# A two-layer decoder trunk: weight blocks added by accumulating transfers, FFN-in by seven products over two quads, FFN-out in parts of 3, 3, 3 and 2

## The chip, the cores and the metric

The kernel runs on one core of one Trainium2 chip. The metric is device time in microseconds (us). Three runs of the kernel before took 2845.32 to 2847.76 us, with a median of 2845.46 us. The execution whose profile is read here took 2846.71 us.

The engines are named as in the profile: PE (TensorE matrix products), PEld (its weight loads), DVE (VectorE), ACT (ScalarE), POOL (GpSimd) and SP (SyncE, which here only issues transfers).

## The reference

Two layers, each on 256 tokens of width 2048:

```python
h = rms_norm(x, g_mix_pre)
proj = h @ w_in                       # 2048 x 11776: pool, conv, q, k, v, swish gate, 3 branch gates
y_pool = pool_mixer(u_pool, ...) @ w_pool_proj
y_conv = conv_module(u_conv, ...) @ w_conv_proj
y_ret = retention(q, k, v, g_ret, ...) @ w_ret_proj
merged = gates[0] * y_pool + gates[1] * y_conv + gates[2] * y_ret
x = x + rms_norm(merged @ w_out, g_mix_post)          # 2048 x 2048
h = rms_norm(x, g_ffn_pre)
a, b = jnp.split(h @ w_ffn_in, 2, axis=-1)            # 2048 x 11264
x = x + rms_norm((jax.nn.silu(a) * b) @ w_ffn_out, g_ffn_post)   # 5632 x 2048
```

All data are 32-bit floats. Nearly all the work is the products with the large weight matrices, and each weight is used once, by 256 tokens.

## The kernel before

**Tiling.** The 256 tokens are two halves (h = 0 and 1) of 128. A weight matrix is cut into chunks of 512 columns, and a chunk into k-tiles of 128 rows. One *product* multiplies one half's k-tile of activations with one k-tile of weights, 128x128 by 128x512, and adds to a PSUM bank. To keep precision, each operand is split into a rounded part and a remainder, so `product` issues three matmuls (L830, L831, L832): activations' high part by weights' high part, low by high, high by low.

**A weight block's way.** A block is two k-tiles (`LOAD`), 128x2x512 floats, 512 KB. `fetch` has SP transfer it into a `raw` buffer (six of them, `RAWBUFS`); `load` has ACT cast it to `whi` (L808) and DVE subtract to get `wlo` (L809); there are seven `whi` and seven `wlo` buffers (`WBLOCKS`). The matmuls read these. The loop at the end of `trunk` runs half 0 ahead of half 1 by up to eight k-tiles (`LAG`), and `load_ahead` loads blocks in the order of the list `items` up to seven blocks beyond where half 1 stands. So the cast of a block waits for a free `whi` buffer, that is, for the last matmul on the block seven places earlier.

**Seven products instead of eight.** For some *quads* (four k-tiles) of a pair of neighbouring chunks n and n+1, the two halves by two row pairs by two chunks form a 2x2 by 2x2 block product. Plainly that is 8 products of each of two k-tiles, 16; by the Winograd form of Strassen's rule it is 7, so 14. `mixed` names the quads, `SEVEN` the kinds of product: b11, b21 and b22 are blocks as they lie in memory, t1 to t4 sums of blocks. b12 is loaded too, but never multiplied itself. Four sums per quad are made on DVE, in place in the `raw` buffers: L788 (t1), L812 (t3), L813 (t2) and L795 (t4). Sums of the activations come from `token_sums`, a small job on DVE and ACT. The partial results are put together on DVE by L868, L870, L875 and L882 for each pair of chunks.

44 pairs of chunks use this, each on one quad: 12 pairs of gate chunks, 2 of the output projection, 20 of FFN-in, 10 of FFN-out.

**FFN.** FFN-in and FFN-out alternate in parts: 3, 4 and 4 column blocks of the hidden layer, each followed by the FFN-out products over those 12, 16 and 16 k-tiles, which add to an accumulator in SBUF (L643, L647, L648).

**Order of the work.** Within an engine the instructions run in the order of the program, which is fixed when it is built. POOL does the adding of branches (L569) and small steps of the norms; it issues no transfers. All transfers are issued by SP.

Of the kernel before, what the change touches and what calls it, by code (L numbers as in the profile page):

```python
# [18 lines left out]
P = 128  # L19
# [20 lines left out]
SLOTS = 24  # L40

# [36 lines left out]
def trunk(ctx: ExitStack, tc: tile.TileContext, x, x_cols, positions, g_mix_post, g_ffn_post, w_in, pool_w,  # L78
# [103 lines left out]
    def pre_norm_quad(h, c, gain, mixed):  # L182
        st["xT", h].append(split(transpose4(x_block(h, c)), gain[:, 4 * c:4 * c + 4]))
        if mixed and c == 3 and h == 1:
            add_sums("sum", "xT", 3)

    def token_sums(lhs, c):

        ts = [st[lhs, h][c] for h in range(2)]
        u = slot([P, 2, 4, P])  # L190
        for h in range(2):
            dve.tensor_tensor(u[:, h], ts[h][:, 0].bitcast(F32), ts[h][:, 1].bitcast(F32), op=ALU.add)
            yield 0.7
        a11, a12, a21, a22 = (u[:, h, 2 * i:2 * i + 2] for h in range(2) for i in range(2))
        s = slot([P, 4, 2, P])
        dve.tensor_tensor(s[:, 0], a21, a22, op=ALU.add)
# [3 lines left out]
        dve.tensor_tensor(s[:, 3], a12, s[:, 1], op=ALU.subtract)  # L200
# [121 lines left out]
    def add_sums(key, lhs, c):  # L322
        jobs.insert(0, [(key, 0), token_sums(lhs, c), 0, True])
# [176 lines left out]
    def ev_rot(key, qd):  # L500
        def f(h, ps):
# [25 lines left out]
            if key == "kT" and qd == 1 and h == 1:  # L527
                add_sums("sum", "xT", 3)
# [29 lines left out]
    def ev_y(b, c):  # L558
        def f(h, ps):
            g = st["sg", h, b, c]  # L560
            if b == 0:
                if c % 2 == 0:
                    st["mt", h, c // 2] = slot([P, 2, NB])
                dve.tensor_tensor(st["mt", h, c // 2][:, c % 2, :], ps, g, op=ALU.mult)
                return
            m = st["mt", h, c // 2][:, c % 2, :]
            t = t2("tb", 2)
            dve.tensor_tensor(t, ps, g, op=ALU.mult)  # L568
            gp.tensor_tensor(m, m, t, op=ALU.add)  # L569
            if b == 2:  # L570
                if c == 0:
                    st["mT", h] = []

                def put():
                    st["mT", h].append(split(transpose4(m)))
                    if h == 1 and c == 0:
                        add_sums("sum", "mT", 0)

                defer(2 * D_T, put)
        return f  # L580
# [38 lines left out]
    def ev_b(first):  # L619
        def f(h, ps, t=None):  # L620
# [9 lines left out]
            def put():  # L630
                hid.append(split(transpose4(u)))
                if first and h == 1:
                    add_sums("sum", "hid", 0)
# [38 lines left out]
    for l in range(DEPTH):  # L672
        wi = w_in[l]

        def gate(b, c, needs=()):
            add(wi, 0, 16, Q_GATE + b * D + c * NB, "xT", ev_gate(b, c), needs)
# [13 lines left out]
        for b in range(3):  # L690
            for c in (0, 2):
                mix(*GATE_QUADS[b])
                for cc in (c, c + 1):
                    gate(b, cc, ("sum", "sum2")[:len(GATE_QUADS[b])])
                for cc in (c, c + 1):
                    project(b, cc)
        for c in range(4):
            if c == 0:
                mix(0)
            add(w_out[l], 0, 16, c * NB, "mT", ev_out(l, c), ("sum",))  # L700
        ends.append(len(chunks))
        parts = ((0, 3), (3, 7), (7, 11))
        for p, (b0, b1) in enumerate(parts):
            last = p == len(parts) - 1
            for j in range(b0, b1):
                if j:
                    mix(3)
                add(w_ffn_in[l], 0, 16, j * NB, "xT", ev_a, ("sum",) if j else ())
                add(w_ffn_in[l], 0, 16, HIDDEN + j * NB, "xT", ev_b(j == b0))
            for c in range(4):  # L710
                if c == 0 or c == 2 and not last:
                    mix(0)
                add(w_ffn_out[l], b0 * 4, (b1 - b0) * 4, c * NB, "hid", ev_ffn(l, c, p, last), ("sum",))
# [14 lines left out]
    while n < len(chunks):  # L728
        ks = list(range(0, chunks[n][2], LOAD))
        if n in mixed:  # L730
            ks = [k for k in ks if k // 4 not in mixed[n]]

            head = max(LAG // LOAD, len(ks) - 1) if len(mixed[n]) == 1 else len(ks)
            for k in ks[:head]:
                plan("", n, k)
            for q in mixed[n][:-1]:
                for kind, d in SEVEN:
                    plan(kind, n, 4 * q + d)
            q = 4 * mixed[n][-1]
            plan("b11", n, q)  # L740
            plan("t1", n, q)
            for k in ks[head:]:
                plan("", n, k)
            plan("b21", n, q + 2)
            plan("b22", n, q + 2)
            for k, kind, kq in zip(ks, ("t2", "t3", "t4"), (q, q, q + 2)):
                plan("", n + 1, k)
                plan(kind, n, kq)
            for k in ks[3:]:
                plan("", n + 1, k)  # L750
# [9 lines left out]
        count[n] = len(items)  # L760
    raws = {}
# [5 lines left out]
    def fetch(i, n=None, k=None):  # L767
        if n is None:
            n, k = items[i][1:]
        w, r0, kt, c0 = chunks[n][:4]  # L770
        r = (r0 + k) * P
        raw = wpool.tile([P, LOAD, NB], F32, name=nm("raw"), tag="raw", bufs=RAWBUFS)
        step = LOAD if i else 1
        for kk in range(0, LOAD, step):
            nc.sync.dma_start(raw[:, kk:kk + step], w[r + kk * P:r + (kk + step) * P, c0:c0 + NB]
                              .rearrange("(k p) n -> p k n", p=P))
# [5 lines left out]
    def load():  # L782
# [3 lines left out]
        if kind == "t1":  # L786
            kept["b12"] = fetch(i, n + 1, k)
            dve.tensor_tensor(kept["b11"], kept["b12"], kept["b11"], op=ALU.subtract)  # L788
            raw = kept["b11"]
        elif kind == "t2":  # L790
            raw = kept["b22"]
        elif kind == "t3":
            raw = kept["b12"]
        elif kind == "t4":
            dve.tensor_tensor(kept["b21"], kept["b21"], kept["b22"], op=ALU.subtract)  # L795
            raw = kept["b21"]
        elif kind == "b22":
            raw = kept[kind] = fetch(i, n + 1, k)
        else:
# [3 lines left out]
            kept[kind] = raw  # L803
# [7 lines left out]
        if kind == "b22":  # L811
            dve.tensor_tensor(kept["b12"], raw, kept["b12"], op=ALU.subtract)  # L812
            dve.tensor_tensor(raw, raw, kept["b11"], op=ALU.subtract)  # L813
# [21 lines left out]
    def mixed_product(kind, n, k, w):  # L835

        kk, last = k % 2, k % 2 == 1 and k // 4 == mixed[n][-1]
        lhs, outs = chunks[n][4], (chunks[n][5], chunks[n + 1][5])
# [23 lines left out]
        elif kind == "b22":  # L862
            product((0, n + 1), "mm0", s_part(3), w, False)
        elif kind == "t2":
            x = bank(s_part(1))
            if last:
# [3 lines left out]
                dve.tensor_tensor(st["sum", 0, n], s, banks["t1", n], op=ALU.add)  # L870
        elif kind == "t3":
            x = bank(s_part(2))
            if last:
                s = st["sum", 1, n]
                dve.tensor_tensor(s, s, x, op=ALU.add)  # L875
        elif kind == "t4":
            y = product((1, n), "mm1", a_part(1), w, last)
            if last:
# [3 lines left out]
                dve.tensor_tensor(s, s, banks["t1", n], op=ALU.add)  # L882

    def multiply(h):
# [6 lines left out]
        else:  # L891
            w, r0, kt, c0, lhs, evac, needs = chunks[n]
            if k == (4 if mixed.get(n, mixed.get(n - 1)) == (0,) else 0):
# [158 lines left out]
```

## Time and profile before

| | |
|---|---|
| runs | 2845.32, 2845.46, 2847.76 us |
| the profiled execution | 2846.71 us, of which the span of its instructions is 2844.9 us |
| granted TensorE clock | 0.999 of full speed |
| PE busy | 2825.8 us (99%) |
| DVE busy | 2257.6 us (79%) |
| ACT busy | 1434.2 us (50%) |
| POOL busy | 104.4 us (4%) |
| read from HBM | 559.11 MB, 199 GB/s over the span with what is written |

The page of the profile gives busy times by engine, the chain of waits (the work that ended last, followed back), and groups of equal instructions, each with its line, engine, operation, `out<-in`, count, busy time, mean of one, and the idle time before it with what ended that. A matmul's record is longer than the distance between two of them, because they overlap; the pace is read from how many lie in a stretch of time.

### The profile page before, as it was taken

The page shows a single profiled execution, that of the slowest core. Times are in us where ns is not written, and L with a number is a line of the kernel's source. Part 1 is how long each engine was busy: PE and PEld are TensorE (multiplying, and loading weights), DVE is VectorE, ACT ScalarE, POOL GpSimd, SP SyncE. Part 2 cuts the span into 40 slices and gives each one's busy share as a digit, 9 for nine tenths or more (in the row PEclk, how much of TensorE's full clock was granted, in tenths as well). Part 3 has the DMA queues.
Part 4 walks back from the last instruction along what each step waited for, and adds up shares of the span by engine and source line. Part 5 has one row for each costly group of instructions (what it writes and reads, how often), then busy time and mean ns, then how long its engine had stood idle before and what let it go on. Part 6 is the DMA issues. An engine that isn't in the chain of part 4 may idle for free.

```text
span 2844.9 us, 34694 instructions
## 1 busy us (share of the span) xinstructions
PE 2825.8 (99%) x12788; PEld 2333.2 (82%) x12788; DVE 2257.6 (79%) x2671; ACT 1434.2 (50%) x1638; POOL 104.4 (4%) x102
## 2 busy tenths in 40 slices
PE   9999999999999999999999999999999999999998
PEld 7888888888888888888888888888888888888887
DVE  6987888776888887787769778787768888887886
ACT  5444544554555554454554455455555554544553
POOL 0000001100100000000000000010000000000000
PEclk9999999999999999999999999999999999999999
DMA  8665655557655665665766655655676565656654
GB/s 306 189 191 172 202 183 188 178 191 259 187 199 200 215 199 172 220 198 192 243 213 186 191 175 177 208 178 180 207 263 189 185 215 188 218 174 201 217 194 166
DMA packets 293898, 569.78 MB, mean 200 GB/s; under 512 B 18272, under 2 KB 21600, under 8 KB 293728
## 3 DMA queue, kind: packets, MB, share of 16 engines
q1 hardware_dynamic: 293728, 567.57, 61.8%
q8 instruction: 100, 1.64, 0.2%
q14 instruction: 70, 0.57, 0.1%
HBM read 559.11 MB, written 8.39 MB: 199 GB/s over the span
## 4 chain that ended last, share of the span: by engine, by line
PE 96%; DVE 3%; ACT 0%; POOL 0%; issue 0%; DMA 0%; SPq 0%; DVEq 0%; POOLq 0%; ACTq 0%
PE mm L832 31%; PE mm L831 31%; PE mm L830 31%; PE tp L143 2%; DVE wlo L809 1%; ACT whi L808 0%; DVE slot L245 0%; PE tp L444 0%; DVE slot L137 0%; DMA raw<-in_w_in 0%; DVE ta L134 0%; DVE ta L464 0%; PE sc L408 0%; PE sc L452 0%; PE sc L434 0%
## 5 line engine op out<-in xcount | busy, mean ns | idle before, releaser
L808 ACT CAST whi<-raw 128x1024 fp32r<-128x1024 f32 (+1 forms) x1157 | 1200.7, 1052 | 1188.3 <-PE mm L831 842.7
L809 DVE TENSOR_TENSOR wlo<-raw,whi 128x1024 fp32r<-128x1024 f32 (+1 forms) x1157 | 1407.7, 1235 | 408.1 <-ACT whi L808 393.1
L830 PE MATMUL mm<-whi,slot 128*128 128x512 f32 x4008 | 1570.4, 392 | 1.2 <-ACT whi L808 0.7
L832 PE MATMUL mm<-wlo,slot 128*128 128x512 f32 x4008 | 1562.5, 390 | 3.6 <-DVE wlo L809 3.5
L831 PE MATMUL mm<-whi,slot 128*128 128x512 f32 x4008 | 1561.4, 390 | 0.7 <-DVE slot L137 0.6
L832 PEld LDWEIGHTS mm<-wlo,slot 128*128 128x128 f32 x4008 | 752.3, 188 | 164.0 <-DVE wlo L809 7.7
L830 PEld LDWEIGHTS mm<-whi,slot 128*128 128x128 f32 x4008 | 752.6, 188 | 155.5 <-ACT whi L808 3.7
L831 PEld LDWEIGHTS mm<-whi,slot 128*128 128x128 f32 x4008 | 752.9, 188 | 154.8 <-DVE slot L137 2.7
L365 DVE SCALAR_TENSOR_TENSOR slot<-slot,par,slot 128x237 f32<-128x237 f32 (+25 forms) x240 | 98.1, 461 | 0.5
L137 DVE TENSOR_TENSOR slot<-tp,slot 128x512 fp32r<-128x512 f32 x60 | 40.8, 685 | 47.4 <-ACT slot L136 47.4
L136 ACT CAST slot<-tp 128x512 fp32r<-128x512 f32 x60 | 35.2, 586 | 84.3 <-PE tp L143 84.3
L569 POOL TENSOR_TENSOR slot<-slot,tb 128x512 f32<-128x512 f32 x32 | 52.9, 1658 | 413.9 <-DVE tb L568 404.7
L237 POOL TENSOR_SCALAR ms_o<-ssq_t 128x1 f32<-128x1 f32 x8 | 1.5, 192 | 1472.8 <-DVE ssq_t L235 1472.8
L788 DVE TENSOR_TENSOR raw<-raw,raw 128x1024 f32<-128x1024 f32 x44 | 53.8, 1223 | 1.3
L813 DVE TENSOR_TENSOR raw<-raw,raw 128x1024 f32<-128x1024 f32 x44 | 53.7, 1221 | 0.9
L812 DVE TENSOR_TENSOR raw<-raw,raw 128x1024 f32<-128x1024 f32 x44 | 53.6, 1218 | 0.3
L795 DVE TENSOR_TENSOR raw<-raw,raw 128x1024 f32<-128x1024 f32 x44 | 53.6, 1218 | 0.2
L625 DVE TENSOR_TENSOR ta<-dt,mm 128x512 f32<-128x512 f32 x40 | 27.3, 683 | 21.5 <-PE mm L832 21.5
L143 PEld LDWEIGHTS tp<-ident,ta 128*128 128x128 f32 x272 | 33.8, 141 | 9.6 <-issue 1.1
L136 ACT CAST slot<-ta 128x512 fp32r<-128x512 f32 x40 | 24.8, 619 | 32.9 <-DVE ta L134 27.6
L143 PE MATMUL tp<-ident,ta 128*128 128x128 f32 x272 | 40.7, 272 | 0.3 <-DVE ta L379 0.2
L148 ACT ACTIVATE tb<-slot 128x512 f32<-128x512 f32 x48 | 30.0, 626 | 21.7 <-DVE slot L648 14.9
(136 smaller groups left out, 948.7 us busy)
## 6 DMA issues: line engine op xcount, KB each, us to landing
raw<-in_w_in SPq DMA_DIRECT2D x367, 512.0 KB, 4.0
raw<-in_w_ffn_in SPq DMA_DIRECT2D x352, 512.0 KB, 4.6
raw<-in_w_ffn_out SPq DMA_DIRECT2D x176, 512.0 KB, 4.7
raw<-in_w_out SPq DMA_DIRECT2D x64, 512.0 KB, 4.4
raw<-in_w_ret_proj SPq DMA_DIRECT2D x32, 512.0 KB, 5.5
raw<-in_w_pool_proj SPq DMA_DIRECT2D x16, 512.0 KB, 5.5
raw<-in_w_conv_proj SPq DMA_DIRECT2D x16, 512.0 KB, 5.7
x<-slot SPq DMA_DIRECT2D x12, 512.0 KB, 4.4
```

The source lines that it names most:

```text
L136: act.copy(t[:, 0], src)
L143: pe.transpose(tp[:, j, :], src[:, j * P:(j + 1) * P], ident)
L365: dve.scalar_tensor_tensor(acc[:, ct, s:], hT[:, ct, :SEQ - s], w[:, TAPS - 1 - s:TAPS - s], acc[:, ct, s:], op0=ALU.mult, op1=ALU.add)
L788: dve.tensor_tensor(kept["b11"], kept["b12"], kept["b11"], op=ALU.subtract)
L795: dve.tensor_tensor(kept["b21"], kept["b21"], kept["b22"], op=ALU.subtract)
L808: act.copy(hi[:, kk:kk + step], raw[:, kk:kk + step])
L809: dve.tensor_tensor(lo[:, kk:kk + step], raw[:, kk:kk + step], hi[:, kk:kk + step].bitcast(F32), op=ALU.subtract)
L812: dve.tensor_tensor(kept["b12"], raw, kept["b12"], op=ALU.subtract)
L813: dve.tensor_tensor(raw, raw, kept["b11"], op=ALU.subtract)
L830: pe.matmul(ps, a[0], w[0], start=first, stop=False)
L831: pe.matmul(ps, a[1], w[0], start=False, stop=False)
L832: pe.matmul(ps, a[0], w[1], start=False, stop=stop)
```

## The change

1. **Sums of weight blocks by transfers.** The four DVE subtractions and the separate load of b12 go. Signs in the block product are turned so that every sum is an addition, and each is made by a transfer from memory that adds to the `raw` buffer in place (`accum_op=ALU.add`), issued by POOL right after the block's `wlo` subtraction. b11's buffer becomes t1, then t2, then t4 by three additions one after the other; b22's buffer becomes t3 by one. `ADDED` says which block of memory is added: (chunk to the right, rows down). The order of the kinds in `items` is new too: b11 and b22 are loaded early, t1, t3, t2 and t4 later.
2. **FFN-in over two quads.** The 20 mixed pairs of FFN-in use quads 2 and 3 (`mix(2, 3)`) in place of quad 3 alone. The results of both quads add up in the same PSUM banks, so the number of combining steps per pair stays.
3. **FFN in parts of 3, 3, 3 and 2.** FFN-out's first three parts use the seven products for both of their pairs of chunks, over quad 0; the last part has none. That is 12 mixed pairs of FFN-out in place of 10.
4. The bank of t3 is read only at t2, with the other combining steps; `token_sums` is finished when the first product of b22 needs it.

```diff
-        if mixed and c == 3 and h == 1:
-            add_sums("sum", "xT", 3)
+        if mixed and c >= 2 and h == 1:
+            add_sums("xT", c)
...
-        parts = ((0, 3), (3, 7), (7, 11))
+        parts = ((0, 3), (3, 6), (6, 9), (9, 11))
...
                 if j:
-                    mix(3)
+                    mix(2, 3)
...
-                if c == 0 or c == 2 and not last:
+                if c % 2 == 0 and not last:
                     mix(0)
...
-    SEVEN = (("b11", 0), ("t1", 0), ("b21", 2), ("b22", 2), ("t2", 0), ("t3", 0), ("t4", 2))
+    ADDED = {"b11": (1, 0), "t1": (1, 2), "t2": (0, 2), "b22": (1, 0)}
...
+            head = LAG // LOAD + 1 - len(quads)
             for k in ks[:head]:
                 plan("", n, k)
+            seven("b11")
+            for k in ks[head:-1]:
+                plan("", n, k)
+            seven("b22")
+            for k in ks[max(head, len(ks) - 1):]:
+                plan("", n, k)
+            seven("t1", "b21", "t3")
+            for i, k in enumerate(ks):
                 plan("", n + 1, k)
+                if i == 0:
+                    seven("t2")
+                if i == min(2, len(ks) - 1):
+                    seven("t4")
...
-        if kind == "t1":
-            kept["b12"] = fetch(i, n + 1, k)
-            dve.tensor_tensor(kept["b11"], kept["b12"], kept["b11"], op=ALU.subtract)
-            raw = kept["b11"]
-        elif kind == "t2":
-            raw = kept["b22"]
-        elif kind == "t3":
-            raw = kept["b12"]
-        elif kind == "t4":
-            dve.tensor_tensor(kept["b21"], kept["b21"], kept["b22"], op=ALU.subtract)
-            raw = kept["b21"]
+        if kind in ("t1", "t2", "t3", "t4"):
+            raw = kept[{"t3": "b22"}.get(kind, "b11"), k // 4]
...
-        if kind == "b22":
-            dve.tensor_tensor(kept["b12"], raw, kept["b12"], op=ALU.subtract)
-            dve.tensor_tensor(raw, raw, kept["b11"], op=ALU.subtract)
+        if kind in ADDED:
+            right, down = ADDED[kind]
+            gp.dma_start(raw, block(n + right, k - k % 4 + down), accum_op=ALU.add)
```

How the change moves instructions, at three places. The numbers behind the names tell one buffer's use from another.

DVE, in a mixed pair of FFN-in of the first layer, before: `raw_9928` is b11, `raw_9949` b12, `raw_10023` b22; L625, L627, L137 and L192 are evacuations and token sums.

```order
L809 TENSOR_TENSOR wlo_9931<-raw_9928,whi_9930 128x1024
L788 TENSOR_TENSOR raw_9928<-raw_9949,raw_9928 128x1024
L625 TENSOR_TENSOR ta_9946<-dt_9650,mm_9793 128x512
L812 TENSOR_TENSOR raw_9949<-raw_10023,raw_9949 128x1024
L627 SCALAR_TENSOR_TENSOR ta_9946<-ta_9946,rstd_6091,sg_9823 128x512
L809 TENSOR_TENSOR wlo_9953<-raw_9928,whi_9952 128x1024
L809 TENSOR_TENSOR wlo_9972<-raw_9969,whi_9971 128x1024
```

The same engine and stage of the changed kernel: `raw_9097` and `raw_9116` are the two quads' b11, here as t1; `raw_9123` and `raw_9151` their b22, here as t3; `raw_9214` and `raw_9220` are b21, `raw_9173` and `raw_9275` plain blocks.

```order
L811 TENSOR_TENSOR wlo_9176<-raw_9173,whi_9175 128x1024
L811 TENSOR_TENSOR wlo_9193<-raw_9097,whi_9192 128x1024
L811 TENSOR_TENSOR wlo_9210<-raw_9116,whi_9209 128x1024
L811 TENSOR_TENSOR wlo_9217<-raw_9214,whi_9216 128x1024
L811 TENSOR_TENSOR wlo_9223<-raw_9220,whi_9222 128x1024
L811 TENSOR_TENSOR wlo_9227<-raw_9123,whi_9226 128x1024
L811 TENSOR_TENSOR wlo_9231<-raw_9151,whi_9230 128x1024
L811 TENSOR_TENSOR wlo_9278<-raw_9275,whi_9277 128x1024
```

DVE only makes `wlo` blocks here; the additions of weight blocks have left its queue.

POOL, in a mixed pair of FFN-in of the changed kernel (before, POOL has no row in these pairs): the eight accumulating transfers of one pair, with the semaphores each waits for. DMAHW are SP's transfers, DMASW POOL's own earlier ones.

```order
L816 DMA raw_7882<-in_w_ffn_in 128x2x512 [waits DMAHW2_49,DMASW2_49,DVE_49]
L816 DMA raw_7889<-in_w_ffn_in 128x2x512 [waits DMAHW3_49,DMASW3_49,DVE_49]
L816 DMA raw_7896<-in_w_ffn_in 128x2x512 [waits DMAHW4_49,DMASW7_49,DMAHW6_49,DMASW6_49,DVE_49]
L816 DMA raw_7939<-in_w_ffn_in 128x2x512 [waits DMAHW5_49,DMAHW7_49,DMAHW1_49,DVE_49]
L816 DMA raw_7882<-in_w_ffn_in 128x2x512 [waits DMASW4_49,DVE_49]
L816 DMA raw_7889<-in_w_ffn_in 128x2x512 [waits DMASW5_49,DVE_49,Activation_49]
L816 DMA raw_7882<-in_w_ffn_in 128x2x512 [waits DMASW0_49,DVE_49]
L816 DMA raw_7889<-in_w_ffn_in 128x2x512 [waits DMASW1_49,DVE_49]
```

Each waits for DVE (the `wlo` of the block it is to add to), and the three on one buffer follow each other.

ACT, in the first pair of FFN-out's second part, before: `raw_8943` is b11, then t1; `raw_8984` and `raw_9013` are a plain block and b21; `raw_9032` is b22, then t2.

```order
L808 CAST whi_8945<-raw_8943 128x1024
L808 CAST whi_8967<-raw_8943 128x1024
L808 CAST whi_8986<-raw_8984 128x1024
L136 CAST slot_9002<-tp_8997 128x512
L808 CAST whi_9015<-raw_9013 128x1024
L855 COPY dt_9008<-mm_8990 128x512
L808 CAST whi_9034<-raw_9032 128x1024
```

The same engine in the second pair of FFN-out's second part of the changed kernel: `raw_8868` is b11, t1, t2 and t4 in turn, `raw_8875` b22 and then t3, `raw_8923` b21; `raw_8959`, `raw_8984` and `raw_8990` are plain blocks of the right-hand chunk.

```order
L810 CAST whi_8870<-raw_8868 128x1024
L810 CAST whi_8877<-raw_8875 128x1024
L810 CAST whi_8902<-raw_8868 128x1024
L810 CAST whi_8925<-raw_8923 128x1024
L860 COPY dt_8918<-mm_8907 128x512
L810 CAST whi_8942<-raw_8875 128x1024
L810 CAST whi_8961<-raw_8959 128x1024
L810 CAST whi_8979<-raw_8868 128x1024
L810 CAST whi_8986<-raw_8984 128x1024
L810 CAST whi_8992<-raw_8990 128x1024
L810 CAST whi_8996<-raw_8868 128x1024
```

Between b11 and t1 there now stands one other block on ACT, between t1 and t2 three, and between t2 and t4 two; each of these distances now holds an accumulating transfer.

More of the change, by code (lines that the diff above doesn't have):

```diff
@@ L617, in ev_a, with ev_b @@
         st["sg", h] = s
-    def ev_b(first):
+    def ev_b(first, last):
         def f(h, ps, t=None):
@@ L631, in put @@
                 hid.append(split(transpose4(u)))
-                if first and h == 1:
-                    add_sums("sum", "hid", 0)
+                if first and h == 1 and not last:
+                    add_sums("hid", 0)
             defer(D_T, put)
@@ L673, in trunk, with gate @@
         wi = w_in[l]
-        def gate(b, c, needs=()):
-            add(wi, 0, 16, Q_GATE + b * D + c * NB, "xT", ev_gate(b, c), needs)
+        def gate(b, c):
+            add(wi, 0, 16, Q_GATE + b * D + c * NB, "xT", ev_gate(b, c))
         def project(b, c):
@@ L693, in trunk @@
                 for cc in (c, c + 1):
-                    gate(b, cc, ("sum", "sum2")[:len(GATE_QUADS[b])])
+                    gate(b, cc)
                 for cc in (c, c + 1):
@@ L760, in trunk @@
         count[n] = len(items)
+    first = {}
+    for i, (kind, n, k) in enumerate(items):
+        if not kind:
+            first.setdefault(n, i)
     raws = {}
@@ L765, in trunk, with block, fetch @@
     done = [0, 0]
-    def fetch(i, n=None, k=None):
-        if n is None:
-            n, k = items[i][1:]
+    def block(n, k, kk=0, count=LOAD):
         w, r0, kt, c0 = chunks[n][:4]
-        r = (r0 + k) * P
+        r = (r0 + k + kk) * P
+        return w[r:r + count * P, c0:c0 + NB].rearrange("(k p) n -> p k n", p=P)
+    def fetch(i):
+        kind, n, k = items[i]
+        n += kind == "b22"
         raw = wpool.tile([P, LOAD, NB], F32, name=nm("raw"), tag="raw", bufs=RAWBUFS)
@@ L774, in fetch @@
         for kk in range(0, LOAD, step):
-            nc.sync.dma_start(raw[:, kk:kk + step], w[r + kk * P:r + (kk + step) * P, c0:c0 + NB]
-                              .rearrange("(k p) n -> p k n", p=P))
+            nc.sync.dma_start(raw[:, kk:kk + step], block(n, k, kk, step))
         raws[i] = raw
@@ L837, in mixed_product @@
         kk, last = k % 2, k % 2 == 1 and k // 4 == mixed[n][-1]
+        if kind == "b22" and not kk:
+            finish({("sum", chunks[n][4], k // 4)})
         lhs, outs = chunks[n][4], (chunks[n][5], chunks[n + 1][5])
@@ L869, in mixed_product @@
                 st["sum", 0, n] = t2("dt", 2)
[L870 to L875, printed above, removed]
+                dve.tensor_tensor(st["sum", 0, n], banks["t1", n], s, op=ALU.subtract)
+                dve.tensor_tensor(s, s, banks["t3", n], op=ALU.add)
         elif kind == "t4":
@@ L892, in multiply @@
             w, r0, kt, c0, lhs, evac, needs = chunks[n]
-            if k == (4 if mixed.get(n, mixed.get(n - 1)) == (0,) else 0):
+            if i == first[n]:
                 finish({(s, q) for s in needs for q in (0, h)})
```

49 lines of the change are left out of this document (20 added, 29 removed).

## The prediction

> **What bounds the kernel now.** I read the page first: busy times, then the chain of waits, then a stretch of pure FFN-in by windows.
>
> ```profile
> PE 2825.8 (99%) x12788; PEld 2333.2 (82%) x12788; DVE 2257.6 (79%) x2671; ACT 1434.2 (50%) x1638; POOL 104.4 (4%) x102
> PE 96%; DVE 3%; ACT 0%; POOL 0%; issue 0%; DMA 0%; SPq 0%; DVEq 0%; POOLq 0%; ACTq 0%
> L830 PE MATMUL mm<-whi,slot 128*128 128x512 f32 x4008 | 1570.4, 392 | 1.2 <-ACT whi L808 0.7
> L831 PE MATMUL mm<-whi,slot 128*128 128x512 f32 x4008 | 1561.4, 390 | 0.7 <-DVE slot L137 0.6
> L832 PE MATMUL mm<-wlo,slot 128*128 128x512 f32 x4008 | 1562.5, 390 | 3.6 <-DVE wlo L809 3.5
> ```
>
> 96% of the chain is PE, and the three matmul groups waited 5.5 us together. So PE's number of matmuls sets the time, and DVE at 79% is next. The means of 390 ns overlap; the pace comes from counting matmuls in a stretch. The windows view, of instructions that touch the PSUM tile mm (columns: stretch, length, PE, PEld, DVE, ACT, clock, DMA share, GB/s):
>
> ```profile
> 1100.00:1200.00 100.00, 100.00 (x443) 82.81 (x442) 14.32 (x21) 1.15 (x2) 1.00 0.65 216
> ```
>
> 443 matmuls in 100 us at full clock is 0.2257 us each.
>
> **The change part by part.** *PE.* A quad done by seven kinds has 14 products where plainly it has 16, so it saves 2 products, 6 matmuls. Before, 44 quads are mixed; after, 12 gate + 2 output + 20x2 FFN-in + 12 FFN-out = 66. That is 22 more, 132 matmuls fewer (3964 per line in the built program for 4008): 132 x 0.2257 = **-29.8 us**.
>
> *DVE, ACT, SP.* The added transfers replace these, each 44 times:
>
> ```profile
> L788 DVE TENSOR_TENSOR raw<-raw,raw 128x1024 f32<-128x1024 f32 x44 | 53.8, 1223 | 1.3
> L813 DVE TENSOR_TENSOR raw<-raw,raw 128x1024 f32<-128x1024 f32 x44 | 53.7, 1221 | 0.9
> L812 DVE TENSOR_TENSOR raw<-raw,raw 128x1024 f32<-128x1024 f32 x44 | 53.6, 1218 | 0.3
> L795 DVE TENSOR_TENSOR raw<-raw,raw 128x1024 f32<-128x1024 f32 x44 | 53.6, 1218 | 0.2
> L809 DVE TENSOR_TENSOR wlo<-raw,whi 128x1024 fp32r<-128x1024 f32 (+1 forms) x1157 | 1407.7, 1235 | 408.1 <-ACT whi L808 393.1
> L808 ACT CAST whi<-raw 128x1024 fp32r<-128x1024 f32 (+1 forms) x1157 | 1200.7, 1052 | 1188.3 <-PE mm L831 842.7
> L648 DVE TENSOR_TENSOR slot<-slot,mm 128x512 f32<-128x512 f32 x32 | 21.8, 683 | 13.8 <-PE mm L832 13.7
> ```
>
> DVE loses 214.7 us and gains 66 casts' remainders (22 quads x 3 more blocks; x 1.235 = 81.5), 24 more adds of FFN-out's fourth part (x 0.683 = 16.4) and some 15 us of combining and token sums for the new pairs and quads: -102 us, 2156 us or 77% of the shorter span. ACT gains 66 x 1.052 = 69 us, to some 53%. Both lie beside PE, and the matmuls waited only 3.5 us for L809, so I book nothing. If that cover went, DVE's queue would be the next wait, at 0.68 to 1.2 us for each thing in front. SP issues 66 loads fewer.
>
> *FFN's parts.* A part of three blocks needs its last hidden quad soon after FFN-out begins. Before, one part per layer is so short; after, all four. This is that place in the trace (timeline, first part's end; brackets: idle before, and who ended it):
>
> ```profile
> 843.15 0.19 PEld L830 LDWEIGHTS mm<-whi,slot 128*128 128x128 f32 x1 [0.18 <-ACT slot L136]
> 843.87 0.19 PEld L831 LDWEIGHTS mm<-whi,slot 128*128 128x128 f32 x1 [0.20 <-DVE slot L137]
> ```
>
> 0.2 us a place on PE; 6 more parts, two halves: **+1 to 2 us**. It would be up to a 1.2 us L809 in front for each of the 12, 15 us in all, if DVE were behind.
>
> *The accumulating transfers.* 26 pairs with one quad have 4, 20 pairs with two have 8: 264, 512 KB each. This trace has no transfer that adds, and none from POOL. Two questions: how long one takes, and what share of the transfer engines.
>
> *How long.* The change adds a wait: ACT's cast of a t block waits for the addition, and behind it in ACT's queue stand the next blocks' casts and the evacuations, which PE then waits for. The room: a cast can start when its `whi` buffer is free. Counted on PE's built order, from the matmul that frees the earlier cast's buffer to the first matmul on the sum there are 55 matmuls for t2 to t4 in a one-quad pair (12.4 us) and 67 in a two-quad pair (15.1 us); FFN-out's b11 to t1 has 55 or 61 (58 on average, 13.1 us), its t1 to t2 61 (13.8 us); all others have 67 or more. In that time fit two casts and two remainders, 2 x (1.05 + 1.24) = 4.6, less 0.45 because the remainder is needed two matmuls later: 4.1 us. So an addition may take 8.3 us in the tightest place, 9.0 and 9.7 in FFN-out's others, 11.0 in FFN-in. The nearest rows, issue to landing of the same 512 KB, and the small POOL steps:
>
> ```profile
> raw<-in_w_in SPq DMA_DIRECT2D x367, 512.0 KB, 4.0
> raw<-in_w_ffn_out SPq DMA_DIRECT2D x176, 512.0 KB, 4.7
> slot<-in_x SPq DMA_DIRECT2D x4, 512.0 KB, 8.8
> L125 POOL TENSOR_SCALAR rstd_a<-ssq_t 128x1 f32<-128x1 f32 x8 | 11.9, 1485 | 82.4 <-DVE ssq_t L210 82.3
> ```
>
> Below: 4.0, as a plain load. Above: 8.8, plus 1.5 for POOL as its slow small step, plus 1.4 for reading 512 KB of buffer at 380 GB/s (below): 11.7. I take the common load: 4.7 + 1.5 + 1.4 = 7.6, under 8.3. **0 us** in the sum, with little to spare.
>
> *What share.* An FFN-in pair takes 180 matmuls, 40.6 us, after the change, with 14 loads and 8 additions. The windows view over all instructions (as above, with POOL before the clock):
>
> ```profile
> 20.00:40.00 20.00, 20.00 (x90) 16.57 (x89) 13.66 (x20) 12.29 (x24) 0.00 (x0) 1.00 1.05 380
> 0.00:40.00 40.00, 37.26 (x148) 26.79 (x149) 24.88 (x37) 21.70 (x38) 0.69 (x6) 1.00 0.98 345
> 2200.00:2400.00 200.00, 200.00 (x895) 165.47 (x894) 169.21 (x175) 105.81 (x112) 0.00 (x0) 1.00 0.60 202
> ```
>
> FFN-in now draws 202 GB/s (16 loads of 0.524 MB per 186 matmuls, 42.0 us, give 200). After: 22 x 0.524 MB in 40.6 us is 284 GB/s if an addition costs the engines as much as a load, well under the 345 to 380 that the start sustains. If it costs two (it must read the buffer too), 30 units ask 387 GB/s, just above what is ever seen. Lower bound one load (nothing gained below it: the bytes must be read), upper two. I take something between, up to 1.5 (26 units, 336 GB/s), which still fits.
>
> By the Trainium skill, "Collectives: The Full Stack", section "The bandwidth ceiling: the fold count and why AG ≠ RS ≠ AR", a reducing transfer runs at half the rate of a copy because both sources are read through one ring. That rule speaks against this change; by it the two-unit case below holds. No row of this trace can show it.
>
> *Sum.* 2846.7 - 29.8 + 1.5 = 2818.4 for an execution like the profiled one; the median lies 1.2 below that one: **2817 us**.
>
> **Rivals.**
>
> *The transfer engines become the bound in FFN-in.* For it: two units per addition ask 387 GB/s against at most 380, and SP's loads already wait for free buffers for most of the span, so a later landing is passed on:
>
> ```profile
> SPq L775 <- DVE wlo L809: 1850.6, 871, 12.2
> ```
>
> Against: copies' 202 GB/s leaves room, and the additions are spread over the pair. Price: 15.7 MB per pair take 41.4 us at 380 GB/s and 45.6 at 345, so 0.8 to 5.0 us too long on 20 pairs: 2833 to 2917, in the middle 2875. This is my case on the slow side; it decides from an addition of 1.9 loads upward.
>
> *An addition takes too long, alone.* It decides from 8.3 us. At 10 us: 1.7 x 26 at t2 to t4, and in FFN-out 1.0 x 12 and 0.3 x 12, some 60 us: 2877. At 11.7: 3.4 x 26 + 2.7 x 12 + 2.0 x 12 + 0.7 x 20 = 159: 2976. At 9: 18 us, 2835. For it: three additions on one buffer follow each other, and POOL's first use as an issuer is unknown. Against: the common landing, 4.0 to 4.7.
>
> *The saving is larger.* With DVE's queue 102 us lighter, small PE stalls go as well; PE's whole idle time is 2844.9 - 2825.8 = 19 us, some of it at the start, so 3 to 8 us at most: 2809 to 2814.
>
> *Both bounds together, or a cost above two loads.* At three loads a pair needs 38 units, 19.9 MB, 57.7 us at 345: +342 us, 3160.
>
> **How the numbers follow.** Forecast (2815 to 2825) 0.50, larger saving 0.05, engines saturated 0.25, one addition too long 0.14, much worse 0.06. 0.2% is 5.7 us, about what a measurement of this kernel can tell from no change: 2839.8 to 2851.2 is no change. Faster: 0.50 + 0.05 + 0.07 of the second + 0.06 of the third = 0.68. Same: 0.05 + 0.03 = 0.08. Slower: the rest, 0.24. The range runs from 2808, under the larger saving, to 2890, which takes in the lower two thirds of the saturated case and half of the long additions; about 2 in 10 lie outside. The forecast's own range is 2812 to 2826.
>
> **What would show it.** PE: 3964 matmuls per line, still some 96% of the chain, 0.226 us apart, about 443 per 100 us in FFN-in. The cast group's idle time ends by PE, not by a transfer. L788, L795, L812 and L813 gone, DVE near 77%. The additions' time to landing under 8.3 us, and 280 to 340 GB/s in the two-quad pairs. I am wrong if the casts' or matmuls' waits name an accumulating transfer, if PE shows fewer than 430 matmuls per 100 us in FFN-in, or if the transfer share there stands at 0.95 or more.

## The result, and the profile after

The changed kernel takes 3182.6 us (median of four runs, 3176.2 to 3184.7) where the kernel before takes 2846.1 (four runs beside them). The ratio is 1.118, with a 95% interval of 1.116 to 1.120: slower by 12%, where 2817 us, 1% faster, was forecast, with 2890 as the upper end.

The page of the changed kernel, in the order of the prediction: busy times, the chain of waits, groups.

```profile
PE 2930.7 (92%) x12656; PEld 2358.5 (74%) x12656; DVE 2151.1 (68%) x2607; ACT 1480.5 (47%) x1708; POOL 420.0 (13%) x366
PE 15%; DMA 13%; issue 7%; DVE 4%; ACT 2%; POOL 1%; DVEq 0%; POOLq 0%; ACTq 0%
L810 ACT CAST whi<-raw 128x1024 fp32r<-128x1024 f32 (+1 forms) x1223 | 1240.9, 1049 | 1423.2 <-PE mm L834 701.1
L833 PE MATMUL mm<-whi,slot 128*128 128x512 f32 x3964 | 1597.8, 404 | 136.8 <-ACT whi L810 132.7
L835 PE MATMUL mm<-wlo,slot 128*128 128x512 f32 x3964 | 1586.4, 400 | 30.0 <-DVE wlo L811 29.2
L144 PE MATMUL tp<-ident,ta 128*128 128x128 f32 x272 | 43.4, 284 | 55.3 <-DVE ta L628 55.3
```

The matmuls are fewer as planned (x3964 a line), and DVE is lighter. But PE is no longer most of the chain: transfers stand beside it. (The shares add up to 42%; the chain could be followed over no more of the span.) PE waits for ACT's cast (L833) and, at the transposes of L144, for an evacuation (L628). These waits, and what the cast waits for, are in the view of waits (us in total, times, longest):

```profile
PE mm L833 <- ACT whi L810: 132.7, 58, 6.2
PE tp L144 <- DVE ta L628: 55.3, 20, 4.0
ACT whi L810 <- DMA raw<-in_w_ffn_in: 271.9, 81, 6.1
ACT whi L810 <- DMA raw<-in_w_ffn_out: 197.2, 34, 9.0
```

The view doesn't tell an addition from a plain load. By the order of the casts, 145 of the 271.9 us stand ahead of casts of sums (139 of them t4) and 127 ahead of casts of plain blocks and b21, which wait for SP's loads; in FFN-out all 197 us stand ahead of sums.

Now the transfers themselves. From the page: the queues (q1 holds SP's loads, q0 POOL's additions; packets, MB, share of the 16 engines' span), the issues (KB, median us to landing) and POOL's time to issue one.

```profile
q1 hardware_dynamic: 275776, 532.96, 49.8%
q0 software_dynamic: 71808, 138.43, 25.9%
raw<-in_w_ffn_in SPq DMA_DIRECT2D x312, 512.0 KB, 5.3
raw<-in_w_ffn_in POOLq DMA_DIRECT2D x160, 512.0 KB, 7.9
raw<-in_w_in POOLq DMA_DIRECT2D x48, 512.0 KB, 7.4
raw<-in_w_ffn_out POOLq DMA_DIRECT2D x48, 512.0 KB, 7.5
L816 POOL DMA_DIRECT2D raw<-in_w_ffn_in x160 | 193.6, 1221 | 800.5 <-DVE wlo L811 689.3
```

532.96 MB are 1016.5 blocks of 0.524 MB, so a load has all 16 engines for 0.498 x 3183.0 / 1016.5 = **1.56 us**; an addition for 0.259 x 3183.0 / 264 = **3.12 us**. That is 2.0 loads. By the Trainium skill, "Collectives: The Full Stack", section "The bandwidth ceiling: the fold count and why AG ≠ RS ≠ AR", a reduction (there a ring step of a collective, ReduceScatter) has half the rate of a copy, as it reads two sources; the 3.12 to 1.56 us here agree with the factor.

Where the time went, by the weight matrix that PE multiplies: from each PE instruction to the next, summed, less 0.2257 us per matmul. I call this the *surplus*; the 61 us of w_in before are mostly the mixers' own small work on PE.

| surplus, us | before | after | difference |
|---|---|---|---|
| w_in (gates) | 61 | 124 | +63 |
| w_out | 6 | 18 | +12 |
| FFN-in | 26 | 181 | +155 |
| FFN-out | 9 | 146 | +137 |

The +367 less the 29.8 us of saved matmuls are the 338 us between the two profiled spans. Three stretches by windows (stretch, length, PE, PEld, DVE, ACT, POOL, clock, DMA share, GB/s): three two-quad pairs of FFN-in, two pairs of FFN-out, and the 3.4 us after one stop of PE.

```profile
969.92:1113.86 143.94, 127.88 (x522) 100.63 (x521) 93.82 (x99) 70.34 (x77) 25.43 (x21) 0.93 0.90 228
1124.93:1198.89 73.96, 61.03 (x239) 47.52 (x238) 43.14 (x47) 29.41 (x31) 7.22 (x6) 0.88 0.70 181
1191.90:1195.30 3.40, 3.36 (x7) 2.27 (x8) 3.40 (x4) 2.75 (x3) 0.00 (x0) 0.50 0.33 88
```

The FFN-in pairs are slow with the transfer engines at 0.90, the FFN-out pairs are slower still with the engines at only 0.70. After the stop the granted clock is 0.50; this lasts from 1190.6 to 1197.4 us. The trace has 48 such stretches, 236.5 us, the last of them behind PE's last instruction (the kernel before has only that one); 333 matmuls there stand some 0.43 us apart, which is 66 of the 367 us.

One chain of FFN-out by the timeline: POOL's issues and ACT's casts of one `raw` buffer (t3's addition is the second POOL row; the casts of b22 and t3 are left out), and the first matmul on t4.

```profile
1163.56 1.20 POOL L816 DMA_DIRECT2D raw<-in_w_ffn_out  x1 [22.26 <-DVE wlo L811]
1165.41 1.20 POOL L816 DMA_DIRECT2D raw<-in_w_ffn_out  x1 [0.64 <-DVE wlo L811]
1172.21 1.20 POOL L816 DMA_DIRECT2D raw<-in_w_ffn_out  x1 [5.60 <-DVE wlo L811]
1182.74 1.20 POOL L816 DMA_DIRECT2D raw<-in_w_ffn_out  x1 [9.32 <-DVE wlo L811]
...
1160.07 1.05 ACT L810 CAST whi<-raw 128x1024 fp32r<-128x1024 f32 x1 [3.67 <-PE mm L834]
1169.61 2.00 ACT L810 CAST whi<-raw 128x1024 fp32r<-128x1024 f32 x2 [5.76 <-PE mm L834]
1180.14 2.94 ACT L810 CAST whi<-raw 128x1024 fp32r<-128x1024 f32 x3 [5.18 <-DMA raw<-in_w_ffn_out]
1190.76 3.89 ACT L810 CAST whi<-raw 128x1024 fp32r<-128x1024 f32 x4 [7.68 <-DMA raw<-in_w_ffn_out]
...
1191.86 0.79 PE L833 MATMUL mm<-whi,slot 128*128 128x512 f32 x1 [5.45 <-ACT whi L810]
```

b11, t1, t2 and t4 are cast at 1160.07, 1169.61, 1180.14 and 1190.76: 9.5 to 10.6 us a link, made of the cast, `wlo`, the issue and the addition. Three links are 30.7 us. b11's cast was 6.8 us ahead of its first matmul (1166.90), and from there to t4's PE had 18.4 us of work: 25.2. t4 comes some 6 us late, PE stops, and then runs at half clock.

### The profile page after: what moved, and what is told of

The parts are those of the page before. It is cut to its first block, busy times and chain, and to the rows that moved or that the text cites. A ratio compares the mean times of both kernels' runs of the same rounds, so it can differ in the third digit from the quotient of the medians.

```text
span 3183.0 us, 35247 instructions
## 1 busy us (share of the span) xinstructions
PE 2930.7 (92%) x12656; PEld 2358.5 (74%) x12656; DVE 2151.1 (68%) x2607; ACT 1480.5 (47%) x1708; POOL 420.0 (13%) x366
## 3 DMA queue, kind: packets, MB, share of 16 engines
q1 hardware_dynamic: 275776, 532.96, 49.8%
## 5 line engine op out<-in xcount | busy, mean ns | idle before, releaser
L811 DVE TENSOR_TENSOR wlo<-raw,whi 128x1024 fp32r<-128x1024 f32 (+1 forms) x1223 | 1479.6, 1232 | 832.0 <-ACT whi L810 796.4
L810 ACT CAST whi<-raw 128x1024 fp32r<-128x1024 f32 (+1 forms) x1223 | 1240.9, 1049 | 1423.2 <-PE mm L834 701.1
L833 PE MATMUL mm<-whi,slot 128*128 128x512 f32 x3964 | 1597.8, 404 | 136.8 <-ACT whi L810 132.7
L834 PE MATMUL mm<-whi,slot 128*128 128x512 f32 x3964 | 1577.1, 398 | 2.9 <-DVE slot L138 2.6
L833 PEld LDWEIGHTS mm<-whi,slot 128*128 128x128 f32 x3964 | 765.8, 193 | 319.4 <-ACT whi L810 164.2
L834 PEld LDWEIGHTS mm<-whi,slot 128*128 128x128 f32 x3964 | 766.0, 193 | 161.3 <-DVE slot L138 5.8
L816 POOL DMA_DIRECT2D raw<-in_w_ffn_in x160 | 193.6, 1221 | 800.5 <-DVE wlo L811 689.3
L816 POOL DMA_DIRECT2D raw<-in_w_in x48 | 58.2, 1213 | 730.5 <-DVE wlo L811 512.1
L816 POOL DMA_DIRECT2D raw<-in_w_ffn_out x48 | 57.8, 1207 | 450.2 <-DVE wlo L811 450.2
L144 PE MATMUL tp<-ident,ta 128*128 128x128 f32 x272 | 43.4, 284 | 55.3 <-DVE ta L628 55.3
L144 PEld LDWEIGHTS tp<-ident,ta 128*128 128x128 f32 x272 | 33.4, 144 | 69.4 <-issue 45.1
L617 ACT ACTIVATE sg<-ta,rstd 128x512 f32<-128x512 f32 x40 | 28.9, 724 | 75.7 <-DVE ta L614 75.7
L137 ACT CAST slot<-tp 128x512 fp32r<-128x512 f32 x60 | 35.1, 585 | 55.1 <-PE tp L144 55.0
L555 ACT ACTIVATE sg<-sg,rstd 128x512 f32<-128x512 f32 x48 | 34.8, 724 | 39.0 <-DVE sg L553 38.8
L649 DVE TENSOR_TENSOR slot<-slot,mm 128x512 f32<-128x512 f32 x48 | 32.7, 682 | 27.7 <-PE mm L835 27.7
```

The lines of the kernel that those rows point to most:

```text
L137: act.copy(t[:, 0], src)
L144: pe.transpose(tp[:, j, :], src[:, j * P:(j + 1) * P], ident)
L555: act.activation(s, ps, ACT.Sigmoid, scale=st["rstd", h])
L810: act.copy(hi[:, kk:kk + step], raw[:, kk:kk + step])
L811: dve.tensor_tensor(lo[:, kk:kk + step], raw[:, kk:kk + step], hi[:, kk:kk + step].bitcast(F32), op=ALU.subtract)
L816: gp.dma_start(raw, block(n + right, k - k % 4 + down), accum_op=ALU.add)
```

## The experiments

Each time below is of a single run unless more are named; the kernel before took 2844.2 to 2847.8 us in all its runs. Two theories at first. **L**: the additions are late, because three stand in series. **B**: they load the transfer engines beyond what these can do.

### 1. Copies in place of additions

The sums are not made here; the order and the bytes read stay.

```diff
-            gp.dma_start(raw, block(...), accum_op=ALU.add)
+            gp.dma_start(raw, block(...))
```

> The changed kernel with plain transfers in place of the adding ones: same issuer (POOL), same places, same bytes read, but each overwrites the buffer. The sums of weight blocks are not made, so the result is not the reference's; the number of products stays. Theory L (an adding transfer is late: it takes about 8 us where a load takes 4 to 5, three of them stand one after the other in a pair, and ACT's queue waits in order): landing falls to 5 to 6 us, a chain of three is 6 to 9 us shorter, and most of the 330 us of PE's idle time goes: 2830 to 2920 us. Theory B (an adding transfer costs the transfer engines two loads, and they are the bound in FFN-in): 22 units in place of 30 per pair, 284 GB/s, also no bound any more: 2815 to 2860. If neither, and POOL's way of issuing is slow by itself, the landing stays at 7 to 8 us and the time above 3100.

2898.9 us. Queue and landing:

```profile
q0 software_dynamic: 38016, 138.43, 15.2%
raw<-in_w_ffn_in POOLq DMA_DIRECT2D x160, 512.0 KB, 5.1
```

0.152 x 2897.1 / 264 = 1.67 us of the engines, 1.07 loads. So 284 of the 337 us belong to the adding (its longer issue, 1.2 us for 0.72, included), not to POOL's issuing by itself. The rest lies in the order, which still has three transfers in series: surplus of FFN-in 60, of FFN-out 59. 25 and 10 us of these are PE's wait at the transposes of L144, once behind each of the 20 two-quad pairs; with additions it is 33 and 22, and in the runs below with one quad it is absent. The time is in L's range and 39 us above B's; but the additions' load and their lateness both went, so the run doesn't tell the two apart.

### 2. to 4. One quad, t4 last, t4's sum on DVE

```diff
-                    mix(2, 3)
+                    mix(3)
```
```diff
-                if i == min(2, len(ks) - 1):
+                if i == len(ks) - 1:
                     seven("t4")
```
```diff
-    ADDED = {"b11": (1, 0), "t1": (1, 2), "t2": (0, 2), "b22": (1, 0)}
+    ADDED = {"b11": (1, 0), "t1": (1, 2), "b22": (1, 0)}
...
+        if kind == "t2":
+            dve.tensor_tensor(raw, kept["b21", k // 4], raw, op=ALU.add)
```

> The changed kernel with FFN-in by seven products on quad 3 alone (46 mixed quads in place of 66, so 120 matmuls more than the change, 27 us; additions and parts 3, 3, 3, 2 kept). An FFN-in pair then has 15 loads and 4 additions, 19 transfers; at two loads for an addition 23 units in place of 30, about 290 GB/s. Theory B: the bound is gone in FFN-in, and the time comes back to 2850 to 2900. Theory L: the chain of three additions is still in every pair, and from t2 to t4 there are only 55 matmuls (12.4 us) in place of 67; only the shortage of raw buffers (two quads hold four of six) is gone. I expect stalls at t4 of 3 to 6 us in each of 44 pairs, 2980 to 3150 us.

> The changed kernel with one edit of the order: t4 stands after the last plain block of chunk n+1, not after its third; traffic is the same to the byte. Theory L: the last addition of a pair gets three plain blocks more, 36 matmuls or 8 us in FFN-in and 4 blocks in the gates, and t4's stall (some 160 us of idle time, with clock loss about 200) goes or shrinks to a third, unless the shortage of raw buffers hands it to the next pair's blocks: 2980 to 3110 us. In FFN-out t4 stands where it was when a pair has at most three plain blocks, so its 64 us stay. Theory B: the transfer engines have as much to do, the wait only moves: 3150 to 3200.

> The changed kernel with the third addition of each chain (t2 to t4) replaced by an addition on DVE from the buffer of b21, which is kept until then; 66 adding transfers fewer, 66 DVE additions of 1.22 us more (80 us of DVE, hidden beside PE). The result is the same. Theory L: a chain has two additions, and t4 needs no landing: t4's stalls (164 us idle, about 200 with the clock) go, but b21's raw buffers are held longer, which may delay the next loads in two-quad pairs: 2900 to 3010 us. Theory B: 26 of 30 units per FFN-in pair, 336 GB/s, an eighth less: only about half of the excess goes, or all of it if the bound lies above 336: 2830 to 3020; the two theories are told apart here by where the stall is left (DMA share near 0.9 for B, t2 for L).

3137.6, 3098.7 and 2944.1 us. The stretch from 1000 to 1200 us, FFN in all three, in the changed kernel, with one quad, and with t4 on DVE (windows, a fence each):

```profile
1000.00:1200.00 200.00, 170.14 (x680) 132.91 (x679) 127.96 (x140) 88.39 (x96) 29.00 (x24) 0.91 0.80 207
```
```profile
1000.00:1200.00 200.00, 182.75 (x770) 145.82 (x769) 129.22 (x139) 86.39 (x93) 22.92 (x19) 0.96 0.75 200
```
```profile
1000.00:1200.00 200.00, 189.27 (x823) 150.17 (x821) 155.00 (x167) 103.90 (x112) 29.10 (x24) 1.00 0.84 223
```

B alone falls: with one quad the engines are less loaded (0.75) and PE still stops; without the third link PE does 823 instructions for 680 while the engines are busier than before, 0.84 (a pair asks them for 26 units there, for 30). L explains the gates: t4 last brings them to 63 us, as before the change. But FFN-in stays (181, then 200). That is a weak test of L there: the edit moves t4 by three plain blocks in a one-quad pair of 16 k-tiles, but by one, 12 matmuls or 2.7 us, in a two-quad pair and in FFN-out (my expectation had three for FFN-in). Better evidence that the two-quad pairs have something of their own is t4 on DVE: FFN-in keeps a surplus of 107 us, and PE's stops there have moved from t4 to plain blocks, b21 and t2.

One rival stands in my expectation for the run with one quad, and no run tests it alone: two quads keep up to four of the six `raw` buffers, which leaves few for plain loads. In the two-quad pairs a right-hand plain block's load lands 1.1 us before its cast (median; 0.9 us in experiment 1, 0.1 us with t4 on DVE, which keeps b21's buffers too), with one quad 4.1 to 10.0 us. In experiment 1 this shortage is there with a surplus of 60, so it doesn't make the loss by itself, but it leaves no room for anything that is late. How much more `raw` buffers would bring is open.

### 5. Both edits: one quad and t4 last

> The changed kernel with both edits already run one by one: FFN-in by seven products on quad 3 alone (3137.6 us alone) and t4 after the last plain block (3098.7 us alone). With two quads, t4 last brought 84 us, nearly all of it in the gates (their matmuls' surplus over 0.2257 us each fell from 124 to 63 us, as before the change) and in FFN-out (146 to 110); FFN-in stayed (181, then 200). If lateness is the one cause (theory L), t4 last should bring about as much here: 3040 to 3070. If in the two-quad pairs the transfer engines are a bound of their own (14 loads and 8 additions at 1.56 and 3.12 us of all 16 engines are 46.8 us, to 40.6 us of PE) and lateness is the cause elsewhere (theory L+B), FFN-in on one quad (15 loads and 4 additions, 35.9 us of engines to 42 of PE) has room, and t4 last frees it as it freed the gates: FFN-in's surplus from 114 to 30 to 50, 2940 to 3000 in all.

2964.7 us, as L and B together had it. Surplus by kernel:

| surplus, us | t4 third | t4 last |
|---|---|---|
| FFN-in, two quads | 181 | 200 |
| FFN-in, one quad | 115 | 40 |
| FFN-out, two / one quad in FFN-in | 146 / 141 | 110 / 109 |

t4's place is worth 75 us in one-quad pairs, where the engines have room, and nothing in two-quad pairs, where it moves by one block for three. In one-quad pairs PE runs almost without a stop at a DMA share of 0.85, and FFN-out stays slow at 0.72:

```profile
924.06:1045.21 121.15, 120.73 (x540) 99.34 (x538) 84.95 (x92) 61.58 (x67) 13.72 (x12) 1.00 0.85 234
1053.84:1126.57 72.73, 62.27 (x246) 47.42 (x245) 40.29 (x44) 28.14 (x31) 8.35 (x7) 0.94 0.72 182
```

### 6. and 7. The engines' load without the additions

Behind each overwriting copy of experiment 1, one more transfer, whose data nobody reads:

```diff
+            spare = dram.tile([LOAD * P, NB], F32, ..., bufs=16)
+            gp.dma_start(spare, raw_rows(n + right, k - k % 4 + down))
```

> The run with overwriting transfers (2898.9 us) with one more transfer behind each of the 264: POOL also copies the same 512 KB from memory to a spare place in memory that nobody reads. So the transfer engines have about as much to do as with additions (a load took 1.6 us of all 16 engines, an addition 3.1; the copy should take some 1.6 or more), but nothing in the program waits for the surplus. The sums are not made, as in that run. Theory L (the additions' lateness on the path, not the engines' load): within 40 us of 2899, 2885 to 2940. Theory B (the engines' load): the loss of the changed kernel comes back, 3050 to 3190. POOL issues two for one (0.7 us each), which may make the overwriting transfers up to 1.5 us later in two-quad pairs.

3171.6 us, but it tests nothing about the pairs: those copies depend on nothing in the program, so they were ordered early; 138 of 264 ran in the first 300 us, the others before 600:

```profile
0.00:300.00 300.00, 207.36 (x725) 144.64 (x725) 139.10 (x262) 82.90 (x110) 79.36 (x148) 0.83 1.01 360
```

725 instructions there, where experiment 1 has 1326. From the 1200th matmul on the distance to experiment 1 hardly changes (285 us, 273 at the end). A surplus transfer has to be tied to its place, here by storing the block's `wlo`:

```diff
+            spare = dram.tile([P, LOAD, NB], F32R, ..., bufs=16)
+            gp.dma_start(spare, lo)
```

> The run with overwriting transfers (2898.9 us) with a store behind each of the 264: POOL writes the block's wlo buffer to a spare place in memory, 512 KB, which nobody reads; it stands at its place, since it needs that buffer's data. The sums are not made. If a store takes the engines as much as a load, a two-quad pair asks them for 30 units of 1.56 us again, 46.8 us, as the additions do, but the chain of transfers is of the short kind. Theory L alone: 2880 to 2930. Theory L+B: FFN-in is held at 46.8 us or more per two-quad pair, 20 times 4 to 6 us more than that run's 43: 2970 to 3030; the DMA share in FFN-in is then 0.95 or more.

3087.8 us; FFN-in's surplus is 197, like the 181 to 200 of the additions. Queue and landing of the copies from the page, then three two-quad pairs by windows:

```profile
q0 software_dynamic: 76032, 276.86, 28.4%
raw<-in_w_ffn_in POOLq DMA_DIRECT2D x160, 512.0 KB, 7.1
```
```profile
936.94:1081.38 144.44, 127.88 (x522) 99.58 (x521) 94.04 (x99) 70.19 (x77) 26.80 (x42) 0.94 0.92 310
```

A copy and a store take 0.284 x 3086.1 / 264 = 3.32 us of the engines, as an addition does 3.12, and the three pairs take 144.4 us, as with additions 143.9. The gates are at 71. So in the two-quad pairs, with their few free buffers, load is enough without an addition, and the copies' landing rises from 5.1 to 7.1 us as its consequence. It acts at the same place: of PE's stops over 0.15 us ahead of FFN-in's matmuls at full clock, 76 of 94 us are at t4 here, and 79 of 82 with additions. So load and lateness are hardly two separate losses in these pairs: the load makes the links longer, and PE stops at the chain's last one. One flaw: a store keeps its `wlo` buffer, and DVE waited for stores 39 times, 49.7 us, of which 17 in FFN-in. I had expected 2970 to 3030: the pairs came to 51 us where I allowed 49, and FFN-out lost 38 us more than in experiment 1, with a share of 0.77 to 0.84.

### 8. to 10. The other parts of the change, sums on DVE and on POOL

All sums on DVE as before, with two quads and the parts of 3, 3, 3, 2; the parts alone; two of four sums on POOL:

```diff
-                    mix(3)
+                    mix(2, 3)
-        parts = ((0, 3), (3, 7), (7, 11))
+        parts = ((0, 3), (3, 6), (6, 9), (9, 11))
```

> The kernel before, with FFN-in over two quads and parts of 3, 3, 3, 2, but all sums of weight blocks on DVE as before and no adding transfer: the same 132 matmuls fewer than before. It tells what the other two parts of the change bring without the transfers. Both theories lay the loss on the transfers, so well under 3183. DVE has in a two-quad pair 30 steps of 1.22 us for blocks and sums and 8.3 us of evacuations and halves, 44.9 us, to PE's 180 matmuls, 40.6 us: DVE would be the bound there, 4.3 us on 20 pairs, 86 us less what the plain stretches take up: 2850 to 2905. A time under 2830 would say that my reckoning of DVE's load is too high.

> The run with all sums on DVE, two quads in FFN-in and parts of 3, 3, 3, 2, timed in rounds, since one look gave 2837.4 to 2845.3 of the kernel before. If that holds, the ratio is 0.997, and the parts of the change beside the transfers make the kernel faster by 0.2 to 0.3%: 2835 to 2840. If the look was luck: 2842 to 2848.

> The kernel before with parts of 3, 3, 3, 2 alone (FFN-in's first quads, the sums on DVE and the order as before): 12 matmuls fewer, 2.7 us, against 1 to 2 us for six more short parts: 2842 to 2847. If short parts cost more than I booked, 2850 or more.

> As the run with all sums on DVE, two quads and parts of 3, 3, 3, 2, but two of the four sums of each quad (t3 and t4) are made by POOL. DVE's work in a two-quad pair falls from 44.9 to 40.0 us beside PE's 40.6; POOL's only large step took 1.55 us for 128x512, so about 3.1 us for one of these, 12.4 us per pair, which POOL has free. If POOL's additions leave DVE's pace alone: 2820 to 2860. If they slow DVE or come too late for t4 (its cast waits 3.1 us instead of 1.2), 2870 or more.

With the sums on DVE 2837.4 us in one run, then 2834.7 as median of five (2833.6 to 2836.3) against 2846.4 (nine runs): ratio 0.996, interval 0.9947 to 0.9974. This version is faster than both kernels, than the one before by 0.4%. FFN-in's surplus is 44 (26 before), FFN-out's 10. 200 us of it:

```profile
1000.00:1200.00 200.00, 198.17 (x885) 162.56 (x884) 196.27 (x205) 111.46 (x119) 0.00 (x0) 1.00 0.59 194
```

DVE is busy for 196.3 of 200 us and still keeps up. My 44.9 us per pair was too high, since DVE's records overlap as PE's do: two steps of 1.22 us take 2.35 us together, the second starting 1.13 after the first (experiment 1):

```profile
1079.04 2.35 DVE L811 TENSOR_TENSOR wlo<-raw,whi 128x1024 fp32r<-128x1024 f32 x2
```

The parts alone: 2844.9 beside 2845.3, no difference.

Two sums on POOL: 2936.4. POOL's additions take 2.4 and 2.6 us, and DVE's remainders become longer, from 1233 to 1350 ns over all:

```profile
L809 DVE TENSOR_TENSOR wlo<-raw,whi 128x1024 fp32r<-128x1024 f32 (+1 forms) x1223 | 1620.6, 1350 | 343.5 <-ACT whi L808 331.5
L812 POOL TENSOR_TENSOR raw<-raw,raw 128x1024 f32<-128x1024 f32 x66 | 159.1, 2411 | 1273.2 <-DVE raw L788 673.4
```

POOL's work isn't free for DVE. FFN-in's surplus rises to 125; how much of that is DVE's pace and how much the later sums, this run doesn't tell.

### 11. Both causes away

One quad, and t4's sum on DVE.

> The changed kernel with FFN-in on quad 3 alone and t4's sum made by DVE from b21's buffer. Both suspected causes are taken away: 15 loads and 3 additions per FFN-in pair are 32.8 us of the engines to 42 us of PE, and no chain has three additions. By both theories most of the loss goes: 2850 to 2900 (12 matmuls fewer than the kernel before, FFN-out's short pairs still with two additions in a row). If it stays above 2950, a third cause is at work, in the order of the work or in POOL's issuing.

2888.7 us: FFN-in's surplus is 31, the gates' 61, FFN-out's 45. So FFN-in and the gates hold no third cause beyond what one quad takes away, which is the shortage of buffers too; FFN-out was left.

### 12. and 13. FFN-out's order

For FFN-out's pairs: b21 ahead of t1, t1 and t3 behind the first plain block of chunk n+1, t2 behind the second, t4 behind the last.

```diff
-            seven("t1", "b21", "t3")
+            late = len(ks) == 4
+            seven(*(("b21",) if late else ("t1", "b21", "t3")))
...
+                if i == 0 and late:
+                    seven("t1", "t3")
-                if i == 0:
+                if i == (1 if late else 0):
                     seven("t2")
```

> The run with one quad in FFN-in and t4's sum on DVE (2888.7 us) with one edit of the order, in FFN-out's pairs alone: b21 before t1, and t1, t3 behind the first plain block of chunk n+1, t2 behind the second, t4 behind the fourth. Its FFN-out matmuls have a surplus of 45 us over 0.2257 each (10 with the sums on DVE). If that is the first link, b11 to t1, which has only b22 in between there, most of it goes: surplus 10 to 25 us, 2853 to 2870 in all. If it is the transfer engines (11 loads and 3 or 4 additions in 31 us), or the evacuations, it stays: 2880 to 2895.

> The same edit of FFN-out's order in the run with one quad and t4 last (2964.7 us), where all three additions of a chain are made by transfers; traffic unchanged. Its FFN-out surplus is 109 us. If FFN-out is held by the chain's length in time, the first link gains 18 matmuls (4 us) and nothing else changes: surplus 60 to 90, 2915 to 2950. If it is held by the transfer engines (11 loads and 4 additions are 29.6 us of engines to 31.1 of PE): no change, 2955 to 2975.

With two additions in the chain (the kernel of experiment 11) 2860.5: FFN-out's surplus falls from 45 to 23. So half of its remainder hung on the order around the first link, b11 to t1 (the edit moves b21 and t2 as well). With three additions (that of experiment 5) FFN-out's surplus stays, 109 and 110, and the 14 us gained (2950.7) are in FFN-in. My expectation for a limit in time, 60 to 90, failed. But the engines aren't the limit in FFN-out either: with one addition more per pair the share is 0.73, less than the 0.78 of the faster run. A fence each, two pairs of FFN-out, two additions and then three:

```profile
1038.51:1095.38 56.87, 55.47 (x246) 45.21 (x244) 44.04 (x47) 29.34 (x31) 5.93 (x5) 1.00 0.78 215
```
```profile
1054.38:1127.99 73.61, 63.14 (x251) 48.91 (x250) 42.22 (x46) 29.17 (x31) 8.35 (x7) 0.93 0.73 185
```

PE's stops went from t1 and the plain blocks back to t4 (59 us there). A slack given to one link was taken from the next: three links of 10.5 us are longer than a pair leaves, wherever the casts stand. That the sum and not the single link decides is my reading of these two runs; longer FFN-out pairs, which would show it directly, weren't run.

## Why the prediction was wrong

- **132 matmuls fewer, -29.8 us: right.** The counts are as predicted. The version with the same 132 fewer and the sums on DVE gains 11.7 us, because FFN-in's surplus rises by 18.
- **DVE and ACT beside PE: right** in size (2151 for 2156 us; 1481 for 1503), and the short parts cost next to nothing.
- **An addition's duration, 7.6 us: right** as a median (7.4 to 8.1 by weight matrix). By place in the pair the medians run from 5.8 to 9.9 us, each within the window that I had allowed there, and PE stopped all the same.
- **"So an addition may take 8.3 us in the tightest place ... 0 us in the sum": the first step that failed.** Each window was measured from the release of a `whi` buffer, as if the cast before it in the chain had been on time. But each link starts where the last ended. The test was to lay three links of 1.05 + 1.24 + 0.3 + 7.6 us, some 31 us, against the distance from b11's cast to t4's first matmul, 25 us in FFN-out. This costs the 63 us in the gates, most of 137 in FFN-out (95 go with t4's sum on DVE), and, with one quad, 75 in FFN-in; in the two-quad pairs PE's stops stand at t4 as well.
- **"I take something between, up to 1.5 (26 units, 336 GB/s), which still fits": the second.** It is 2.0, the upper bound. And the capacity was wrong: I took 345 to 380 GB/s from the first 40 us, but the row of 2200 to 2400 us that I quoted has a share of 0.60 at 202 GB/s, which is 337 GB/s at a share of 1. At 1.56 us a unit even 26 units are 40.6 us, all that a pair has; 30 are 46.8. FFN-in's surplus rose by 155 us, 7.8 on each of 20 pairs, where the rival had 0.8 to 5.0; experiment 7 shows that load of this size is enough for it, but not how much of it the few free buffers and the two-quad order add.
- **The rivals.** Engines as a bound (0.25) and late additions (0.14) were both named, each alone and each at about 2875. Both came, each larger, and together. "Both bounds together" had 0.06, with a price for three loads per addition alone; that its 3160 is near the time is luck, since an addition cost two.
- **The clock wasn't in any sum.** After its stops PE ran at a granted clock of 0.50, for 3.4 to 10.2 us at a time; 66 us. The Trainium skill, "TensorE: Matmul & The Clock Gate", section "What's actually happening", has the clock at half after an idle window of about 3.4 us. Here less was enough: in the 3.4 us ahead of each of the 47 stretches amid the work PE stood idle for 2.0 to 3.4 us.

What I had said would show me wrong did: the casts wait for additions (145 us in FFN-in), PE shows 363 instructions per 100 us in the three two-quad pairs above for 443, and the share in the stretches of two-quad pairs alone is 0.90 to 0.95.

## What to carry to other kernels

When a step is replaced by a longer one that hides, add up the whole dependent chain, from its first input to its last use, and lay it against the time PE takes over that distance; windows between neighbours that each fit can sum to a chain that doesn't. Reckon the transfer engines in engine time per transfer (share x span / count), not in GB/s of some busy stretch: a transfer that adds cost 2.0 loads here, so it spares DVE 1.1 us at the price of 3.1 us of all engines. And when PE begins to wait, count the half pace after the stops as well.

## What the runs showed of the hardware beyond that

- POOL needs 1.2 us to issue an adding transfer of 512 KB and 0.72 us for a plain one.
- In the gates the first addition on a buffer lands after 5.8 us (t1) and 5.9 (t3), the second and third after 8.0 and 7.9 (t2, t4). Why is open.
- A plain transfer issued by POOL lands as fast as SP's loads (5.1 to 4.8 us in FFN-in of experiment 1), and takes the engines 1.07 times as long.
- A store of 512 KB beside them took the engines 1.65 us (3.32 less 1.67).
